# One full-width product per chunk operator in a bidirectional scan, instead of two half-width ones

## The chip, the cores and the metric

The kernel runs on one core of one Trainium2 chip. The metric is the time on the device in microseconds, from the program's first instruction to its end; several runs of the same program are taken and their median is compared.

## The reference, cut to what matters

One layer of a diffusion backbone is computed for 128 context tokens and 2048 latent tokens of width 1024. The input is normalised, modulated and multiplied by one wide input projection. Half of the channels (8 heads of 64) go through a recurrence with a 64 x 64 state per head, run once forward and once backward; the other half go through a short gated convolution; both halves meet in one output projection. The recurrence is what the change touches:

```python
def step(S, inp):
    r_t, w_t, k_t, v_t, kk_t, a_t = inp
    s_kk = jnp.einsum('bdhij,bdhj->bdhi', S, kk_t)
    S = (S * w_t[..., None, :] - s_kk[..., :, None] * (kk_t * a_t)[..., None, :]
         + v_t[..., :, None] * k_t[..., None, :])
    return S, jnp.einsum('bdhij,bdhj->bdhi', S, r_t)
...
s_final, ys = lax.scan(step, s0.astype(f32), xs)
```

## The kernel before, in words

The kernel has three phases. The first projects the inputs and writes the scan's operands to scratch memory. The second, the scan, is the one of interest. The third applies the output projection; its beginning is woven into the scan's end.

The scan works on chunks of 64 tokens. Within a chunk the recurrence is turned into matrix products, so that the state is carried from chunk to chunk by one product with an operator matrix of 128 x 128 for each head. A stage holds two groups, one per direction (`gi` and `d` are 0 for forward, 1 for backward), each of 8 chunks of one pair of heads. There are 17 stages; stage 15 is the context stage, whose groups hold two chunks of each of the four pairs.

For each stage and direction, in the names that the profile shows:

- `load_rr` (L998) and `load_sv` fetch operands and values; `load_stk` (L951) fetches one stack's lower half, tokens of 8 chunks for two heads, into partitions 0 to 63 of `stf`, `stg` or `sth`. These loads are issued on SyncE's queue, one DMA of 256 KB per stack in ordinary stages (L956) and four smaller ones per stack in the context stage (L959).
- `product` (L1021, tiles psGm, psQm, psFm) multiplies operands in 64 x 64 pieces; VectorE masks the results; GpSimd inverts small triangular matrices (`inverse`, L1081, tile zt); `merge` and `solve` (psU, psW, psX) build the rest of the inverse from them.
- `gcopies` (L1151) and `solve` (L1172) are ScalarE's writes of the stacks' upper halves, partitions 64 to 127.
- `operator` (L1174) multiplies the two stacks of a direction. One call makes the operators of two chunks and two heads in one tile, psE: for each of the four, two matmuls (L1186), one for each half of the 128 weight columns, writing partitions 0 to 63 and 64 to 127 of the result. A second call, "Ev", masks psE into E on VectorE (L1191).
- `state` (L1199, L1217, psS) applies E to the carried state with 64-column halves as weights; `scaled` (L1243) scales the new state on VectorE; the next chunk's psS waits for it. `outputs` and `finish` (psT at L1315, L1319, L1321) normalise and gate the output, with loads of `sg` and `w` (L1283) on SyncE.

A stack has two blocks (`b`, identity or copied rows), two heads (`h`) and eight chunks (`u`) of 64 tokens (`t`). Each direction has one `stf` tile, and one `stg` and one `sth` tile that alternate from stage to stage. The forward direction takes its weights from `stf` and its moving operand from `stg` or `sth`; the backward direction the other way round.

The order of instructions on TensorE, VectorE and ScalarE in the scan is written out by hand in the tables `SEQ` and `LATE`; GpSimd's and SyncE's orders are made by the scheduler. The words in these tables name a step, the two digits of its half and quarter, the direction and the stage distance: E000+1 is an operator product of the next stage. The change leaves the tables as they are.

In the order of TensorE's program there are 136 operator products in 82 runs. Of these runs 65 begin right after psS or psT and 17 after another tile; 64 end right before psS or psT.

The functions that the diff touches:

Of the kernel before, what the change touches and what calls it, by code (L numbers as in the profile page):

```python
# [6 lines left out]
F32 = mybir.dt.float32  # L7
# [808 lines left out]
def phase2(K):  # L816
    nc, tc, A, S = K.nc, K.tc, K.A, K.S
    V, G, P, T = nc.vector, nc.gpsimd, nc.scalar, nc.tensor
    D = nc.sync.dma_start
    MF, MG, ME = (0, 1), (0, 1), (2, 3)  # L820
    B = Ctx()
    O = Ctx()
    O.scaled = None

    def setup_first():

        O.r0 = Pool(K, "p2r0", "right")
        O.rI = Pool(K, "p2rI", "right")
        O.r1 = Pool(K, "p2r1", "right")
        O.pm = Pool(K, "p2m", "right", 2, PSUM)  # L830
        B.msk = O.r0.tile([128, 4, 128], F32, name="msk")
        B.mkg = O.r0.tile([128, 2, 128], F32, name="mkg")
        for i, j in enumerate((0, 2, 4, 5)):
            D(B.msk[:, i], A["msk"][:, j, 0:128])
        for i, j in enumerate((1, 3)):
            D(B.mkg[:, i], A["msk"][:, j, 64:192])
        B.I2 = O.r0.tile([128, 64], F32, name="I2")
        D(B.I2[:], A["i2"])
        B.idt = O.r0.tile([128, 128], F32, name="idt2")
        D(B.idt[:], A["idt"])  # L840
        B.hm = O.r0.tile([128, 2], F32, name="hm")
        D(B.hm[:], A["cst"][:, 514:516])
        B.ph = O.r0.tile([128, 3], F32, name="ph")
        D(B.ph[:], A["cst"][:, 516:519])
        B.slots = []
        for i in range(2):
            new_slot(O.r0)
        B.rr = ring(O.r1, 2, [128, 5, 8, 64], "rr", presetR)

    def new_slot(pool):  # L850
        i = len(B.slots)
        B.slots.append([tuple(pool.tile([128, 8, w], F32, tag=f"{n}{i}{d}", name=f"{n}{i}{d}", bufs=1) for n, w in (("F", 128), ("GA", 128), ("Q", 64))) for d in range(2)])
# [8 lines left out]
    def setup_rest():  # L861
        O.l0 = Pool(K, "p2l0", "left")
        O.l1 = Pool(K, "p2l1", "left")
        O.pS = Pool(K, "p2S", "left", 4, PSUM)
        O.p2 = Pool(K, "p2s", "left", 2, PSUM)
        O.r2 = Pool(K, "p2r2", "right")
        new_slot(O.r2)
        cp = O.l0
        vec = cp.tile([128, 4], F32, name="vec2")
        D(vec[:], A["vec"][:, V_GW:V_GW + 4])  # L870
        B.gwh = cp.tile([128, 4], F32, name="gwh")
        V.tensor_scalar(B.gwh[:], vec[:], 0.5, None, ALU.mult)
        B.geps = cp.tile([128, 1], F32, name="geps")
        V.memset(B.geps[:], 64e-5)
        B.pc = cp.tile([64, 2, 8, 34], F32, name="pc")
        for d in range(2):
            D(B.pc[:, d], S[f"pc{d}"].rearrange("(e c) n -> c e n", c=64))

        B.fs = ring(O.l1, 2, [128, 2, 2, 8, 64], "stf", presetS)
        B.gs = ring(O.l1, 2, [128, 2, 2, 8, 64], "stg", presetS)  # L880
        B.gs2 = ring(O.r2, 2, [128, 2, 2, 8, 64], "sth", presetS)
        B.zb = O.l1.tile([128, 16, 64], F32, name="zb")
        zero(B.zb)

    def ring(pool, n, shape, name, init=None):
        l = [pool.tile(shape, F32, name=f"{name}{i}") for i in range(n)]
        if init:
            for t_ in l:
                init(t_)

        def get():
            l.append(l.pop(0))
            return l[-1]
        get.tiles = l
        return get

    def copy(k, dst, src, negate=False):
        if negate:
            if k in ON_DVE:
                V.tensor_scalar(dst, src, -1.0, None, ALU.mult)  # L900
            else:
                P.activation(dst, src, AF.Copy, scale=-1.0)
        else:
            (V.tensor_copy if k in ON_DVE else P.copy)(dst, src)

    def zero(t_):
        G.memset(t_[:], 0.0)
# [6 lines left out]
    def presetS(t_):  # L914
        for hd in range(2):
            V.tensor_copy(t_[0:64, 0, hd], B.I2[0:64].unsqueeze(1).broadcast_to((64, 8, 64)))

    def tl(shape, tag, b, pool=None, dt=F32):
        return (pool or O.l0).tile(shape, dt, tag=tag, name=f"{tag}_{K.u()}", bufs=b)
# [29 lines left out]
    H0, H1, FULL = slice(0, 64), slice(64, 128), slice(0, 128)  # L949

    def load_stk(t_, g, k):  # L951

        p, c0 = g.units[0]
        src = S[f"ops{g.d}"][k]
        if p == g.units[-1][0]:
            D(t_[0:64, 1].rearrange("c h u t -> c h (u t)"), src[p * 128:p * 128 + 128, c0 * 64:(c0 + 8) * 64].rearrange("(h c) t -> c h t", h=2))  # L956
            return
        for i in range(4):
            D(t_[0:64, 1, :, 2 * i:2 * i + 2].rearrange("c h u t -> c h (u t)"), src[i * 128:i * 128 + 128, c0 * 64:(c0 + 2) * 64].rearrange("(h c) t -> c h t", h=2))  # L959

    def half(g, n):

        h = n if g.d == 0 else 1 - n
        return slice(h * 4, h * 4 + 4)
# [28 lines left out]
    def psum(name, s, shape):  # L993

        pool, tag = pool_of(name, s)
        return pool.tile(shape, F32, tag=tag, name=f"ps{name}_{s}_{K.u()}")
# [132 lines left out]
    def load_fs(s, st, gi):  # L1129

        g = st.g[gi]
        g.fs = B.fs.tiles[gi]
        load_stk(g.fs, g, 2)

    def load_gs(s, st, gi):

        g = st.g[gi]
        g.gs = (B.gs2 if s % 2 and s < NST - 3 else B.gs).tiles[gi]
        load_stk(g.gs, g, 1)
# [34 lines left out]
    def operator(name, s, st, gi):  # L1174

        g = st.g[gi]
        n, h2 = (int(c) for c in name[-3:-1])
        us = half(g, n)
        k = (h2 if g.d == 0 else 1 - h2) * 2
        if name[:2] != "Ev":  # L1180
            lt, rt = (g.fs, g.gs) if g.d == 0 else (g.gs, g.fs)
            pe = g.ps[name] = psum(name, s, [128, 2, 2, 128])
            for i in range(2):
                for hd in range(2):
                    for b, r in enumerate((H0, H1)):
                        T.matmul(pe[r, i, hd, :].rearrange("p (b t) -> p b t", b=2), lt[:, b, hd, us.start + k + i], rt[:, :, hd, us.start + k + i], start=True, stop=True)  # L1186
            return
        if n not in g.E:
            g.E[n] = tl([128, 4, 2, 128], f"E{n}{gi}", 1)
        pe = g.ps.pop("E" + name[-3:])  # L1190
        V.tensor_tensor(g.E[n][:, k:k + 2].rearrange("p a b c -> p (a b) c"), pe[:].rearrange("p a b c -> p (a b) c"),  # L1191
                        B.msk[:, ME[g.d]].unsqueeze(1).broadcast_to((128, 4, 128)), ALU.mult)
# [138 lines left out]
    def ending(name, s, st, gi):  # L1331
# [3 lines left out]
        if st.fin is not None:  # L1335
            next(st.fin, None)

    DO = dict(Gm=product, Qm=product, Fm=product, Ge=m_evict, Qe=m_evict, Fa=m_evict, Fe=m_evict, dg=diag, ab=turn, zi=begin, pre=pre, I=inverse,
              zr=zrows, zd=zrows, c0=zcopies, c1=zcopies, U=merge, bu=merge, W=merge, n=merge, gh=gcopies, X=solve, Xc=solve,
              E=operator, Ev=operator, S=state, sv=scaled, y=outputs,  # L1340
              fw=ending, fr=ending, fq=ending, fm=ending, T=ending, fy=ending, fa=ending)
    LOAD = dict(L=load_rr, gsL=load_gs, fsL=load_fs, svL=load_sv)
# [40 lines left out]

    def main():
        setup_rest()
        for b, n, t in order_of(range(-3, 0)):
            K.body = b
# [222 lines left out]
def build(nc, tc, A, outs):  # L1610
    K = Ctx()
    K.nc, K.tc, K.A = nc, tc, A
    n = [0]

    def u():
        n[0] += 1
        return n[0]

    K.u = u
    K.S = dict(outs)  # L1620
    for name, shape in {**SCR, **SCR2, "gate": (2, 1024)}.items():
        if name not in K.S:
            K.S[name] = tc.dram_tile(list(shape), F32, name=f"scr_{name}")[:]
    K.S["wsp"] = tc.dram_tile([34, 128, 2, 8, 128], F32, name="scr_wsp")[:]
    phase3(K)
    phase2(K)
    phase1(K)
    K.main()
# [18 lines left out]
```

## Time and profile before

| what | value |
|---|---|
| median of 3 runs | 1623.51 us (1619.18 to 1625.04) |
| the profiled execution | 1630.73 us |
| its span, first to last instruction | 1629.0 us |
| mean granted TensorE clock | 0.972 |
| scan, first stretch | 970 to 1345 us of the span |
| scan, its end with the context stage | 1345 to 1430 us |
| VectorE busy in the span | 70% |
| ScalarE, GpSimd busy in the span | 47%, 34% |

How to read the rows that follow: in the table of busy times a row is a stretch in microseconds, its length, and for each engine the busy time and, in brackets, the number of records; after them stand the granted clock, the share of the DMA engines and GB/s. In the chain and the timeline a row is a start, a length, the engine, the line and the tile, and how many records were merged into it. A form such as 128\*64 says how many rows and columns of weights a matmul uses. A float32 matmul leaves two records. The ends of matmuls are modelled, so starts and the ends of groups tell more than one record's length. "issue" is time in which an engine waited for nothing that the profile shows.

### The profile page before, as it was taken

How to read it: one execution, taken by the hardware profiler on the slowest of the kernel's cores; microseconds unless marked ns; L12 is line 12 of the kernel's file. 1: busy time of each engine (PE TensorE's matmuls, PEld its weight loads, DVE VectorE, ACT ScalarE, POOL GpSimd, SP SyncE). 2: the span in 40 equal slices, each digit the busy share in tenths (PEclk: the TensorE clock that was granted, in tenths of full speed). 3: DMA queues.
4: the chain of work that ended last, by engine and by line, in shares of the span. 5: the costliest groups of instructions: out<-in, count | busy, mean ns of one | idle time of the engine just before them, and what ended most of it. 6: DMA issues, size and time to landing. Idle time of an engine off the chain costs nothing.

```text
span 1629.0 us, 41750 instructions
## 1 busy us (share of the span) xinstructions
PE 1515.5 (93%) x17364; PEld 1402.4 (86%) x17364; DVE 1139.8 (70%) x1960; ACT 773.2 (47%) x1494; POOL 557.5 (34%) x961
## 2 busy tenths in 40 slices
PE   5899989999999999999999988999899897699998
PEld 2799989999999998999999987888788786578786
DVE  5899994764999636369975257897888886446533
ACT  4466652433555213145631047877687677322222
POOL 0033330001333000023315417787678866113221
PEclk8899999999999999999999979999999998799999
DMA  9559998663878765358886545565667645355442
GB/s 373 202 149 270 262 270 308 222 223 109 215 219 233 236 230 178 114 163 233 258 241 225 207 110 143 159 194 147 158 179 203 152 139 162 103 166 175 138 147 96
DMA packets 204589, 313.94 MB, mean 193 GB/s; under 512 B 58088, under 2 KB 147560, under 8 KB 190320
## 3 DMA queue, kind: packets, MB, share of 16 engines
q1 hardware_dynamic: 168816, 311.13, 61.9%
q10 hardware_dynamic: 35584, 0.14, 1.4%
q8 instruction: 136, 2.23, 0.6%
q14 instruction: 53, 0.43, 0.1%
HBM read 208.05 MB, written 103.17 MB: 191 GB/s over the span
## 4 chain that ended last, share of the span: by engine, by line
PE 64%; DVE 16%; DMA 9%; issue 6%; ACT 2%; SPq 1%; POOL 1%; ACTq 0%; DVEq 0%; POOLq 0%
PE psE L1186 6%; PE psu L1501 4%; PE psS L1217 3%; PE psu L1502 3%; PE psu L1503 3%; DMA scr_ops<-xs 2%; PE psFm L1019 2%; PE psX L1168 2%; PE mmb L182 2%; PE mmb L184 2%; PE mmb L183 2%; PE mmu L182 2%; PE mmu L184 2%; PE mmu L183 2%; PE mmgb L183 2%
## 5 line engine op out<-in xcount | busy, mean ns | idle before, releaser
L1091 POOL TENSOR_TENSOR zt<-zt,ztmp 128x30 f32<-128x30 f32 (+7 forms) x510 | 209.5, 411 | 39.7
L1088 POOL TENSOR_TENSOR ztmp<-ab,zt 128x60 f32<-128x60 f32 (+7 forms) x255 | 134.8, 529 | 104.5 <-DVE ab L1079 80.6
L1217 PE MATMUL psS<-sv,E 128*64 128x64 f32 x2176 | 103.1, 229 | 25.0 <-DVE so L1243 13.5
L1217 PEld LDWEIGHTS psS<-sv,E 128*64 128x64 f32 x2176 | 84.9, 140 | 43.9 <-issue 15.4
L410 POOL TENSOR_TENSOR sh<-rawl 128x384 f32<-128x384 f32 (+1 forms) x48 | 46.7, 991 | 210.6 <-ACT rawl L401 210.6
L1191 DVE TENSOR_TENSOR E<-psE,msk 128x512 f32<-128x512 f32 x136 | 91.0, 684 | 18.6 <-PE psE L1186 18.2
L1243 DVE TENSOR_TENSOR sv<-psS,pc 64x128 f32<-64x128 f32 x254 | 64.2, 275 | 45.1 <-PE psS L1217 43.6
L1566 POOL TENSOR_TENSOR z<-z,x 128x512 f32<-128x512 f32 x32 | 42.7, 1338 | 151.0 <-DVE z L1560 87.5
L1172 ACT ACTIVATE stf<-psX 64x512 f32<-64x512 f32 x136 | 80.4, 591 | 14.7 <-PE psX L1168 12.4
L434 POOL TENSOR_TENSOR hsl<-sq,hsh 128x384 fp32r<-128x384 f32 (+1 forms) x24 | 33.2, 1383 | 142.7 <-ACT hsh L429 137.0
L182 PE MATMUL mmg<-h,w 128*128 128x384 f32 (+1 forms) x216 | 70.8, 328 | 0.0
L183 PE MATMUL mmg<-h,w 128*128 128x384 f32 (+1 forms) x216 | 70.7, 327 | 0.0
L184 PE MATMUL mmg<-h,w 128*128 128x384 f32 (+1 forms) x216 | 70.6, 327 | 0.0
L182 PE MATMUL mmb<-h,w 128*128 128x384 f32 (+1 forms) x192 | 63.2, 329 | 6.0 <-ACT w L150 3.4
L182 PE MATMUL mmv<-h,w 128*128 128x384 f32 (+1 forms) x192 | 63.7, 332 | 3.8 <-ACT lf L665 3.1
L219 POOL TENSOR_TENSOR hslq<-ssq,hshq 128x384 fp32r<-128x384 f32 (+1 forms) x4 | 4.8, 1206 | 175.9 <-ACT hshq L218 112.0
L182 PE MATMUL mmc<-h,w 128*128 128x384 f32 (+1 forms) x192 | 63.7, 332 | 0.1
L184 PE MATMUL mmc<-h,w 128*128 128x384 f32 (+1 forms) x192 | 63.1, 329 | 0.3 <-DVE w L154 0.3
L184 PE MATMUL mmv<-h,w 128*128 128x384 f32 (+1 forms) x192 | 63.2, 329 | 0.0
L183 PE MATMUL mmv<-h,w 128*128 128x384 f32 (+1 forms) x192 | 63.1, 329 | 0.0
L183 PE MATMUL mmc<-h,w 128*128 128x384 f32 (+1 forms) x192 | 63.0, 328 | 0.0
L182 PE MATMUL mmu<-h,w 128*128 128x384 f32 (+1 forms) x192 | 62.7, 327 | 0.3 <-DMA w<-scr_wsp 0.3
(311 smaller groups left out, 5061.1 us busy)
## 6 DMA issues: line engine op xcount, KB each, us to landing
w<-scr_wsp SPq DMA_DIRECT2D x68, 1024.0 KB, 5.6
scr_wsp<-w SPq DMA_DIRECT2D x34, 1024.0 KB, 6.1
rr<-scr_ops SPq DMA_DIRECT2D x32, 1024.0 KB, 5.7
scr_ops<-xs SPq DMA_DIRECT2D x160, 192.0 KB, 6.2
wr<-in_win SPq DMA_DIRECT2D x34, 512.0 KB, 6.6
x<-in_x SPq DMA_DIRECT2D x17, 512.0 KB, 3.9
wadas<-in_wada SPq DMA_DIRECT2D x8, 1024.0 KB, 13.7
sv<-scr_vt SPq DMA_DIRECT2D x32, 256.0 KB, 3.7
```

Of the source, the lines that this page charges most:

```text
L182: T.matmul(ps[:, :n], w[:, 0, k], hh[:, 0, k, :n], start=k == 0, stop=False)
L183: T.matmul(ps[:, :n], w[:, 0, k], hh[:, 1, k, :n], start=False, stop=False)
L184: T.matmul(ps[:, :n], w[:, 1, k], hh[:, 0, k, :n], start=False, stop=k == 7)
L1088: G.tensor_tensor(tv, ab[:, j:j + 2, j + 2:32].unsqueeze(1).broadcast_to((128, kn, 2, n)), zt[:, :kn, j:j + 2].unsqueeze(3).broadcast_to(( ...
L1091: G.tensor_tensor(zt[:, :kn, j + 2:32], zt[:, :kn, j + 2:32], tv[:, :, r], ALU.subtract)
L1172: P.activation(g.fs[64:128, :, hd, e::2], g.ps["X"][e][hr_].rearrange("p a (b t) -> p b a t", b=2), AF.Copy, scale=-1.0)
L1186: T.matmul(pe[r, i, hd, :].rearrange("p (b t) -> p b t", b=2), lt[:, b, hd, us.start + k + i], rt[:, :, hd, us.start + k + i], start=True, ...
L1191: V.tensor_tensor(g.E[n][:, k:k + 2].rearrange("p a b c -> p (a b) c"), pe[:].rearrange("p a b c -> p (a b) c"), B.msk[:, ME[g.d]].unsquee ...
L1217: T.matmul(g.sp[i // 4][r, q, hd, :], g.E[n][:, k, hd, r], g.sv[:, u, hd, :], start=True, stop=True)
L1243: V.tensor_tensor(dst, g.sp[i // 4][0:64, q], B.pc[0:64, d, 2 * p:2 * p + 2, c:c + 1].broadcast_to((64, 2, 64)), ALU.mult)
L1501: T.matmul(ps[:], mh[:, n], hi[:, cs], start=start and n == 0, stop=False)
L1502: T.matmul(ps[:], mh[:, n], lo[:, cs], start=False, stop=False)
```

## The change

For each operator, one matmul with all 128 weight columns takes the place of the two with 64. Its weights must lie in one run of 128 elements per partition, so the tile that holds weights (`stf` of the forward direction, `stg` and `sth` of the backward one) is laid out anew: the two blocks of 64 tokens of a chunk stand side by side. A new helper, `stacks`, makes the tiles and hands out views with the old order of axes, so that the writers need no change. The lower half of such a tile is loaded in pieces of 256 bytes instead of 2 KB, by two DMAs, one per head. In the context stage all stacks, of either layout, are loaded by twice as many DMAs.

```diff
@@ -876,9 +876,9 @@
-        B.fs = ring(O.l1, 2, [128, 2, 2, 8, 64], "stf", presetS)
-        B.gs = ring(O.l1, 2, [128, 2, 2, 8, 64], "stg", presetS)
-        B.gs2 = ring(O.r2, 2, [128, 2, 2, 8, 64], "sth", presetS)
+        B.fs = stacks(O.l1, "stf", 0)
+        B.gs = stacks(O.l1, "stg", 1)
+        B.gs2 = stacks(O.r2, "sth", 1)
@@ -893,6 +893,19 @@
+    def stacks(pool, name, lhs):
+
+        c = Ctx()
+        c.tiles = []
+        for i in range(2):
+            if i == lhs:
+                t_ = pool.tile([128, 2, 8, 2, 64], F32, name=f"{name}{i}")[:].rearrange("p h u b t -> p b h u t")
+            else:
+                t_ = pool.tile([128, 2, 2, 8, 64], F32, name=f"{name}{i}")[:]
+            presetS(t_)
+            c.tiles.append(t_)
+        return c
@@ -952,11 +965,16 @@
         src = S[f"ops{g.d}"][k]
+        if g.d == (k == 1) and p == g.units[-1][0]:
+            for h in range(2):
+                D(t_[0:64, 1, h], src[p * 128 + h * 64:p * 128 + h * 64 + 64, c0 * 64:(c0 + 8) * 64].rearrange("c (u t) -> c u t", t=64))
+            return
         if p == g.units[-1][0]:
             D(t_[0:64, 1].rearrange("c h u t -> c h (u t)"), src[p * 128:p * 128 + 128, c0 * 64:(c0 + 8) * 64].rearrange("(h c) t -> c h t", h=2))
             return
         for i in range(4):
-            D(t_[0:64, 1, :, 2 * i:2 * i + 2].rearrange("c h u t -> c h (u t)"), src[i * 128:i * 128 + 128, c0 * 64:(c0 + 2) * 64].rearrange("(h c) t -> c h t", h=2))
+            for h in range(2):
+                D(t_[0:64, 1, h, 2 * i:2 * i + 2], src[i * 128 + h * 64:i * 128 + h * 64 + 64, c0 * 64:(c0 + 2) * 64].rearrange("c (u t) -> c u t", t=64))
@@ -1182,8 +1200,7 @@
                 for hd in range(2):
-                    for b, r in enumerate((H0, H1)):
-                        T.matmul(pe[r, i, hd, :].rearrange("p (b t) -> p b t", b=2), lt[:, b, hd, us.start + k + i], rt[:, :, hd, us.start + k + i], start=True, stop=True)
+                    T.matmul(pe[:, i, hd, :].rearrange("p (b t) -> p b t", b=2), lt[:, :, hd, us.start + k + i].rearrange("p b t -> p (b t)"), rt[:, :, hd, us.start + k + i], start=True, stop=True)
```

On TensorE, this is the middle of the scan, stage 8's operator products (psE, with the moving operand and the weights behind the arrow) between state products of two directions and the next psGm; "64x128" is the result's partitions by columns. Before:

```order
L1186 MATMUL psE_8_1439_14058<-stf_9633,stg_9639 64x128 x8
L1217 MATMUL psS_0_0_14069<-sv_13461,E_1434_13996 64x64 x4
L1217 MATMUL psS_1_4_13967<-sv_13069,E_1403_13611 64x64 x4
L1186 MATMUL psE_8_1441_14088<-stg_9638,stf_9632 64x128 x8
L1217 MATMUL psS_1_4_13967<-sv_13069,E_1403_13611 64x64 x4
L1217 MATMUL psS_0_0_14069<-sv_13461,E_1434_13996 64x64 x4
L1186 MATMUL psE_8_1445_14116<-stf_9633,stg_9639 64x128 x8
L1186 MATMUL psE_8_1447_14127<-stg_9638,stf_9632 64x128 x8
```

And after, at the same place, where lines of the code have moved by 17:

```order
L1203 MATMUL psE_8_1439_13817<-stf_9635,stg_9641 128x128 x4
L1234 MATMUL psS_0_0_13824<-sv_13254,E_1434_13755 64x64 x4
L1234 MATMUL psS_1_4_13730<-sv_12880,E_1403_13388 64x64 x4
L1203 MATMUL psE_8_1441_13843<-stg_9638,stf_9632 128x128 x4
L1234 MATMUL psS_1_4_13730<-sv_12880,E_1403_13388 64x64 x4
L1234 MATMUL psS_0_0_13824<-sv_13254,E_1434_13755 64x64 x4
L1203 MATMUL psE_8_1445_13867<-stf_9635,stg_9641 128x128 x4
L1203 MATMUL psE_8_1447_13874<-stg_9638,stf_9632 128x128 x4
```

Every step stands where it stood; a product is four matmuls over all 128 partitions instead of eight over halves.

On SyncE, the queue of an ordinary stage, from the stack loads to the next stage's operands. Before:

```order
L956 DMA stg_9639<-scr_ops_59 64x2x512
L956 DMA stf_9633<-scr_ops_59 64x2x512
L956 DMA stf_9632<-scr_ops_57 64x2x512
L956 DMA stg_9638<-scr_ops_57 64x2x512
L1283 DMA w_14384<-scr_q 128x512
L1009 DMA rr_8377<-scr_ops_57 128x4x512
L1009 DMA rr_8378<-scr_ops_59 128x4x512
```

And after:

```order
L970 DMA stg_9641<-scr_ops_59 64x8x64 x2
L973 DMA stf_9635<-scr_ops_59 64x2x512
L970 DMA stf_9632<-scr_ops_57 64x8x64 x2
L973 DMA stg_9638<-scr_ops_57 64x2x512
L1300 DMA w_14117<-scr_q 128x512
L1027 DMA rr_8377<-scr_ops_57 128x4x512
L1027 DMA rr_8378<-scr_ops_59 128x4x512
```

The two stacks that hold weights take two issues each, ahead of the w and rr loads.

On SyncE again, the context stage after the change, where before 16 loads at L959, of the form 64x2x128, stood in the stretch from the first stf row to the second group of sv rows:

```order
L977 DMA stf_9632<-scr_ops_57 64x2x64 x4
L960 DMA sv_16598<-scr_vt 64x4x128 x2
L977 DMA stf_9632<-scr_ops_57 64x2x64 x4
L977 DMA stg_9638<-scr_ops_57 64x128 x8
L1342 DMA scr_mixT<-sg_16416 128x512
L977 DMA stf_9635<-scr_ops_59 64x128 x3
L1300 DMA sg_16674<-scr_sg 128x512
L977 DMA stf_9635<-scr_ops_59 64x128 x5
L977 DMA stg_9641<-scr_ops_59 64x2x64 x8
L960 DMA sv_16844<-scr_vt 64x4x128 x2
L957 DMA sv_16865<-scr_vt 64x8x128
L1300 DMA w_16962<-scr_q 128x512
```

The 32 loads stand ahead of the sv and w loads; behind them come the loads of the output projection's weights (L1466 before, L1483 after).

## The prediction

> **What bounds the kernel now.** I read the page first, then the chain of waits, then the scan's stretch of both, then single pieces of TensorE's work there. The profiled execution took 1630.73 us, of which the span is 1629.0; the median of the runs shown is 1623.51. Differences are worked out inside the profiled span and put on the median.
>
> ```profile
> PE 64%; DVE 16%; DMA 9%; issue 6%; ACT 2%; SPq 1%; POOL 1%; ACTq 0%; DVEq 0%; POOLq 0%
> ```
>
> TensorE carries 64% of the chain that ended last. The change sits in the scan, so the scan's own rows count: the busy table of its two stretches, for all work and then for the operator products (tile psE) alone, and the chain's shares in the first stretch.
>
> ```profile
> 970.00:1345.00 375.00, 339.75 (x9320) 307.66 (x9320) 313.91 (x627) 279.58 (x555) 286.30 (x642) 0.97 0.60 164
> ```
>
> ```profile
> 970.00:1345.00 375.00, 123.67 (x1920) 107.10 (x1920) 79.00 (x118) 0.97 0.60 164
> 1345.00:1430.00 85.00, 21.14 (x258) 18.50 (x256) 12.03 (x18) 0.84 0.49 143
> ```
>
> ```profile
> by line: PE psE L1186 20.9%; PE psS L1217 13.6%; issue 8.1%; PE psX L1168 7.6%; PE psFm L1019 7.6%; PE psGm L1019 5.9%; DVE E L1191 4.6%; PE psU L1116 3.4%; DVE GA L1035 3.4%; PE psQm L1019 3.2%; DVE ab L1060 2.9%; DVE y L1262 2.8%; DVE sv
> ```
>
> TensorE is busy 339.75 of 375 us; VectorE, 313.91, is next. The products have 1920 + 258 records (two stand in both stretches), twice the program's 1088 matmuls: a float32 matmul leaves two records. They hold 20.9% of 375 = 78.4 us of the chain. What one chunk stage looks like on the chain:
>
> ```profile
> 1209.45 0.62 PE psS L1217 x16
> 1210.07 0.88 PE psE L1186 x16
> 1210.94 0.26 PE psS L1217 x8
> ...
> 1214.21 1.02 PE psE L1186 x16
> 1215.24 0.47 PE psS L1217 x16
> 1215.70 0.88 PE psE L1186 x16
> 1216.58 0.46 PE psS L1217 x16
> 1217.04 3.50 PE psE L1186 x64
> 1220.54 0.46 PE psS L1217 x16
> 1221.00 0.88 PE psE L1186 x16
> 1221.88 1.03 PE psGm L1019 x32
> ```
>
> Start, length, work. TensorE runs without a gap, so here a longer operator product lengthens the kernel one for one. A product of 16 records takes 0.88 us, four in a row 3.50, so 0.875 each: 78.4 of the 120 x 0.875 = 105 us of the first stretch, three quarters, lie on the chain.
>
> **The halved matmuls.** The diff replaces eight matmuls of 64 weight columns per product by four of 128, each streaming the same 128 columns. That saves time only if the two 64-column matmuls now run one after the other. They don't, by a row of its line's group and three of the timeline:
>
> ```profile
> L636 PE MATMUL psgate<-gaterow,sel x4: 591/592/592, 611.1 to 664.0; 128*2 128x512 f32 x4
> ```
>
> ```profile
> 611.09 1.02 PE L636 MATMUL psgate<-gaterow,sel 128*2 128x512 f32 x2
> ```
>
> ```profile
> 547.58 1.06 PE L212 MATMUL psgr<-wgate,scp 128*32 128x512 f32 x6
> ```
>
> ```profile
> 1209.89 1.05 PE L1186 MATMUL psE<-sth,stf 128*64 128x128 f32 x16
> ```
>
> psgate is one float32 matmul alone: its two records, 0.59 us each, end 1.02 us after the first began, so a record of 512 columns occupies its part of the array for 0.43 us. psgr has three times as many records, in three column parts, in 1.06 us: the parts work side by side. By the same rate a record of 128 columns should take 0.43 / 4 = 0.107 us, and 0.875 / 16 = 0.055 is half of that: the two column halves of a product already run together, at 0.109 per pair.
>
> A full-width record then takes 0.107 to 0.11 for its columns. Its weights are twice as wide, so the load beside it could become the limit. The nearest row is the transposes of v, 128 x 128 weights under 128 columns:
>
> ```profile
> 94.60 0.49 PE L504 MATMUL psv<-idt,ov 128*128 128x128 f32 x3
> ```
>
> ```profile
> L504 PE MATMUL psv<-idt,ov x68: 270/272/273, 94.6 to 837.8; 128*128 128x128 f32 x68
> ```
>
> Three take 0.49, the last one 0.27 of it, so they follow each other every 0.11 us with their loads hidden. A product after the change is 8 records x 0.109 = 0.875 us, as now. I take 0 for this edit; its ends are one record at half that (rival 1) and a load that isn't hidden (rival 3).
>
> The Trainium skill's "TensorE: Matmul & The Clock Gate", section Measured speedup vs the span model, states 2.38 times for three column tiles, not 3. By that, as an estimate, a pair would take 3 / 2.38 = 1.26 full records, and the change would save a fifth of 136 x 0.875 = 119 us, 25 us before any loss. The rows above disagree: three parts of psgr took 1.06 us where one alone took 1.02.
>
> **The borders.** Today psE, psS and psT all work in halves (128*64). After the change psE uses the whole array, and each border with psS or psT becomes a change of shape. What that costs stands in the chain. Sixteen psS records take 0.47 after psE and 0.62 after psX (64*64): 0.15 to leave. A product takes 0.88 after psS and 1.02 after psGm: 0.14 to enter in halves. Entering the full array is dearer:
>
> ```profile
> 1418.56 0.43 PE psa L1501
> 1418.99 0.23 PE psa L1502
> ```
>
> These are the first two full-width records after a psE: 0.43 against 0.23, so 0.20 to enter. The Trainium skill's "TensorEngine Tiling (Array Packing)", section Key Properties, says a change of tiling mode drains the engine and gives no figure; by a drain that costs the same both ways, taken at the 0.15 of leaving, the sum below would be 129 x 0.15 = 19.4. The rows make entering dearer, which I read as the wider first load standing exposed, and the measurement decides.
>
> In TensorE's order there are 82 runs of products; 65 begin after psS or psT, 64 end before one, and 17 begin after another shape, where 0.14 is paid already and 0.20 will be. So 65 x 0.20 = 13.0, 64 x 0.15 = 9.6, 17 x 0.06 = 1.0: 23.6 us of TensorE time. Three quarters of products lie on the chain, but the rest has little slack beside an engine busy 339.75 of 375; between 0.75 and 1 I take 0.85: **20 us**.
>
> **Instructions.** 1088 records and their 1088 weight loads go. TensorE's gaps marked "issue" in the scan's first stretch:
>
> ```profile
> PE psFm L1019 <- issue: 6.8, 7, 1.6
> PE psQm L1019 <- issue: 6.6, 3, 3.2
> PE psE L1186 <- issue: 4.4, 4, 1.4
> PE psS L1217 <- issue: 4.2, 4, 1.9
> ```
>
> 22.0 us in 18 gaps of about a microsecond. Those between 1195 and 1290 us, counted over the trace's TensorE records, start whole multiples of 256 records apart, so I take them for instruction loads that came late. 13.4 us stand before the quick psFm and psQm records, which stay; of the 8.6 before psE and psS I take a quarter: **-2 us**, ends -12 and 0.
>
> **The loads.** Each stage's two weight stacks come as two DMAs in 256-byte pieces instead of one in 2 KB pieces, and the context stage's 16 loads become 32. Rows of the trace's table of transfers (size, us to landing), of SyncE's queue, of TensorE and of VectorE:
>
> ```profile
> stf<-scr_ops SPq DMA_DIRECT2D x32, 256.0 KB, 5.6
> ```
>
> ```profile
> 1221.21 1.58 SPq L956 DMA_DIRECT2D stf<-scr_ops  x2
> ...
> 1334.43 0.58 SPq L959 DMA_DIRECT2D stf<-scr_ops  x1
> ...
> 1352.33 0.54 SPq L1283 DMA_DIRECT2D w<-scr_q  x1
> ```
>
> ```profile
> 1234.77 1.05 PE L1186 MATMUL psE<-stg,stf 128*64 128x128 f32 x16
> ```
>
> ```profile
> 1357.14 0.67 DVE L1321 TENSOR_TENSOR sg<-sg,w 128x512 f32<-128x512 f32 x1
> ...
> 1367.29 1.05 DVE L1099 STREAM_TRANSPOSE zr<-zt 128x512 f32<-128x512 f32 x1 [2.56 <-POOL zt L1091]
> ```
>
> In an ordinary stage two more issues of 0.6 put 1.2 us ahead of the w and rr loads. The stf loads go out at 1221 to 1223, the product that needs the first direction's starts at 1234.77; with landings of 5.6 us some 6 us of cover are left, and pieces twice as slow would use it up. I take 0, upper end 1 us a stage for 16 stages. In the context stage 16 more issues, 9.6 us less some 3 of waiting in that queue, fall between 1334 and 1352. Behind them stand w, which L1321 needs, and two output-weight loads, whose splitting runs on VectorE just ahead of the zr transpose at 1367.29. L1321 would slip from 1357 to about 1365 and zr by 3 to 5 us; behind zr the chain goes on. I take **+3**, ends 0 and 9.
>
> The preset copies, ScalarE's writes into the new layout (still runs of 64 elements) and the moving operands keep their sizes: 0.
>
> **Sum:** 20 - 2 + 3 = 21 us, so 1651.7 against the profiled 1630.73 and **1644.5 us** on the median.
>
> **Rivals.**
> 1. The halves don't really overlap, or a full-width float32 record is quicker than 0.107: each record then costs 0.055, 1088 x 0.054 = 59 us go, 50 on the chain, and with the borders the time is 1623.5 - 50 + 21 = 1595. It decides at 0.09 a record (21 us = 0.85 x 1088 x 0.023). For it: no row has a full-width float32 product of many columns. Against it: psgate and psgr. Chance 0.06.
> 2. The borders are absorbed: only half lies on the chain (12 us), and thinner instruction traffic takes half of the 22 us of issue gaps (-11): 1624, with 1615 to 1632 around it. For: issue holds 8.1% of the chain. Against: the gapless stage above. Chance 0.13.
> 3. Full-width weight loads can't run beside the record before: 0.107 more for each of 1088, 116 us, 99 on the chain: 1743. Against it: psv's spacing. Chance 0.05. The same page of the Trainium skill, section What overlaps and what doesn't, says loads overlap only where the row groups differ, which here they never do; the psv row contradicts it.
>
> **How the numbers follow.** The forecast has 0.76. Its own range: low 0.6 of the borders, -6 for instructions and 0 for loads, 1623.5 + 8 = 1632; high 23.6, 0, 9 and 12 for loads of ordinary stages, 1668. To hold the time 8 times in 10 the range takes in most of rival 2: 1626 to 1668, with rivals 1 and 3 outside. This kernel's measurement tells about 0.5%, 8 us, from no change. Faster by more: rival 1 and a little of rival 2, 0.08. Same: the rest of rival 2, 0.11. Slower: the forecast and rival 3, 0.81.
>
> **What the profile after would show.** 1088 psE records as 128*128, TensorE's count down to about 16276; a product alone between psS about 1.08 us on the chain, four in a row 3.70, the psS behind them 0.62: the border step right. Products of 0.5 us: rival 1. Products of 1.7: rival 3. Issue gaps under 12 us: rival 2. The context stage's loads ending 6 to 10 us later relative to their start, with L1321 or zr waiting: the load step. Wrong altogether if psE's length between psS stays 0.88 and the time still moves.

## The result, and the profile after

The changed kernel took 1637.76 us in the median of 8 runs (1632.55 to 1644.67), the kernel before 1625.77 us on the same chip (8 runs, 1619.18 to 1629.4): a ratio of 1.0075 with a 95% interval of 1.0053 to 1.0098, or 12 us more (9 to 16). By the half per cent that this measurement can tell, the change is slower. The profiled executions spanned 1629.0 us before and 1638.0 after, 9 us apart; the first took 5 us more than its kernel's median, the second 2 us more.

The chain of the changed kernel, shares by engine: TensorE rose from 64% to 70%.

```profile
PE 70%; DVE 13%; DMA 8%; issue 5%; ACT 2%; SPq 2%; ACTq 0%; DVEq 0%
```

One stage of it on the chain (start, length, work), the counterpart of the stage in the prediction:

```profile
1265.81 0.62 PE psS L1234 x16
1266.42 1.09 PE psE L1203 x8
...
1276.33 0.62 PE psS L1234 x16
1276.95 3.77 PE psE L1203 x32
1280.72 0.61 PE psS L1234 x16
1281.33 1.09 PE psE L1203 x8
1282.42 1.09 PE psGm L1037 x32
```

A product alone between psS now takes 1.09 us (0.88 before), four in a row 3.77 (3.50), the psS behind a product 0.61 to 0.62 (0.47). So the borders are there.

The kernels are compared below over the **ordinary stages**, here from the first to the 112th eviction of an operator on VectorE. There are eight evictions a stage, so these are the first 14 stages; the loads of the context stage (stage 15) are issued behind them. The busy table over that stretch, before and then after (length, then busy time and count of TensorE, weight loads, VectorE, ScalarE and GpSimd, then TensorE's granted clock):

```profile
977.67:1327.48 349.81, 315.61 (x8764) 285.80 (x8762) 296.88 (x592) 261.74 (x519) 271.73 (x602) 0.98 0.61 166
```

```profile
977.78:1335.43 357.65, 330.83 (x7866) 294.13 (x7862) 300.46 (x593) 261.85 (x519) 259.33 (x602) 0.99 0.61 163
```

TensorE is busy 15.2 us longer, but the stretch is only 7.8 longer: its idle time fell from 34.2 to 26.8 us.

What came behind that. First SyncE's queue in the changed kernel while it issues the context stage's loads, then what VectorE waited for there (us in total, times, longest), then VectorE's work that waited and the transpose zr on which the chain goes on:

```profile
1341.95 2.69 SPq L977 DMA_DIRECT2D stf<-scr_ops  x4
...
1361.13 7.39 SPq L977 DMA_DIRECT2D stg<-scr_ops  x8
1368.63 1.19 SPq L960 DMA_DIRECT2D sv<-scr_vt  x2
1369.94 0.58 SPq L957 DMA_DIRECT2D sv<-scr_vt  x1
1370.62 0.57 SPq L1300 DMA_DIRECT2D w<-scr_q  x1
1371.28 0.86 SPq L1483 DMA_DIRECT2D woraw<-in_wout  x2
```

```profile
DVE sg L1338 <- DMA w<-scr_q: 8.3, 1, 8.3
```

```profile
1374.59 0.69 DVE L1338 TENSOR_TENSOR sg<-sg,w 128x512 f32<-128x512 f32 x1 [8.28 <-DMA w<-scr_q]
...
1382.16 1.04 DVE L1117 STREAM_TRANSPOSE zr<-zt 128x512 f32<-128x512 f32 x1
```

The load of w goes out 35.2 us behind the 112th eviction (1335.43); before it was 24.9 (1352.33 behind 1327.48). VectorE stands 8.3 us at L1338, where it didn't wait before (L1321), and zr starts 46.7 us behind that eviction instead of 39.8. So another 6.9 us were lost up to zr.

This zr is the 17th and last, one for each stage, so it belongs to stage 16, the ordinary stage behind the context stage; the expectations below call it the context stage's, and the 112th eviction the last of the 16 ordinary stages. In VectorE's order it stands ahead of the context stage's evictions, so these slip with it. The context stage's own zr starts 16.9 us behind the 112th eviction before and 17.9 after.

Then the start of the output projection, where the tile psa is computed, before and then after:

```profile
1418.40:1441.20 22.80, 20.31 (x95) 15.38 (x92) 10.02 (x18) 5.43 (x11) 1.38 (x2) 0.93 0.65 197
```

```profile
1432.10:1449.50 17.40, 17.40 (x90) 13.87 (x89) 10.07 (x18) 5.14 (x10) 0.11 (x1) 1.00 0.79 242
```

For the same 72 records of psa, and a few of its neighbours, the kernel before needed 22.8 us at a clock of 0.93, the changed one 17.4 at 1.00. That is where some 5 us came back: from the 129th eviction to the end it took 222.1 us before and 216.5 after. Three views of the kernel before show what it lost there: what TensorE waited for within psa, ScalarE's work that it waited for, and the stretch right behind:

```profile
PE psa L1501 <- ACT mhc L1488: 2.5, 1, 2.5
```

```profile
1435.35 0.62 ACT L1488 CAST mhc<-mxc 128x512 fp32r<-128x512 f32 x1 [6.68 <-DMA mxc<-scr_mixT]
```

```profile
1437.40:1440.60 3.20, 3.20 (x9) 2.52 (x8) 1.58 (x3) 0.00 (x0) 1.28 (x1) 0.50 0.58 166
```

TensorE waits for a cast on ScalarE, which waits for the load of mxc, and then runs 3.2 us at half the clock. In the changed kernel it does neither. So the spans' 9.0 us are 7.8 in the ordinary stages, 6.9 from there to zr, about -6 behind that, and a rest under half a microsecond.

### The profile page after: what moved, and what is told of

Same layout as the page of the kernel before. It is cut to its first block, busy times and chain, and to the rows that moved or that the text cites. A ratio compares the mean times of both kernels' runs of the same rounds, so it can differ in the third digit from the quotient of the medians.

```text
span 1638.0 us, 39662 instructions
## 1 busy us (share of the span) xinstructions
PE 1535.5 (94%) x16276; PEld 1415.5 (86%) x16276; DVE 1141.5 (70%) x1960; ACT 772.9 (47%) x1494; POOL 547.8 (33%) x961
## 4 chain that ended last, share of the span: by engine, by line
PE 70%; DVE 13%; DMA 8%; issue 5%; ACT 2%; SPq 2%; ACTq 0%; DVEq 0%
PE psE L1203 8%; PE psS L1234 5%; PE psu L1518 4%; PE psu L1519 3%; PE psu L1520 3%; PE psX L1186 2%; PE psGm L1037 2%; PE mmb L182 2%; PE mmb L184 2%; PE psFm L1037 2%; PE mmb L183 2%; PE mmc L182 2%; PE mmc L183 2%; PE mmc L184 2%; PE mmu L184 1%
## 5 line engine op out<-in xcount | busy, mean ns | idle before, releaser
L1109 POOL TENSOR_TENSOR zt<-zt,ztmp 128x30 f32<-128x30 f32 (+7 forms) x510 | 197.1, 386 | 39.8
L1234 PE MATMUL psS<-sv,E 128*64 128x64 f32 x2176 | 103.1, 231 | 28.8 <-DVE so L1260 13.1
L1234 PEld LDWEIGHTS psS<-sv,E 128*64 128x64 f32 x2176 | 79.8, 139 | 53.4 <-DVE sv L1260 15.0
L1583 POOL TENSOR_TENSOR z<-z,x 128x512 f32<-128x512 f32 x32 | 42.7, 1338 | 146.2 <-DVE z L1577 99.4
L434 POOL TENSOR_TENSOR hsl<-sq,hsh 128x384 fp32r<-128x384 f32 (+1 forms) x24 | 35.6, 1485 | 141.6 <-ACT hsh L429 141.6
```

The lines of the kernel that those rows point to most:

```text
L1109: G.tensor_tensor(zt[:, :kn, j + 2:32], zt[:, :kn, j + 2:32], tv[:, :, r], ALU.subtract)
L1234: T.matmul(g.sp[i // 4][r, q, hd, :], g.E[n][:, k, hd, r], g.sv[:, u, hd, :], start=True, stop=True)
```

## The experiments

My theory after this: the borders cost TensorE about what I had priced, a thinner instruction stream gave part of it back, and the context stage's loads cost as much again. Rivals: the borders are simply absorbed by slack, or the loads cost everything.

A single profile scatters: for the three kernels with unchanged operator products in the old order the ordinary stages took 349.8, 340.0 and 351.8 us. So besides the length two parts are given. All TensorE records of the stretch are taken by their starts; where two follow each other by more than 0.3 us, all but 0.11 of it counts as **gap**, and the rest is **continuous work**. The table sets all kernels side by side (e7 has no row, because its one profiled execution took 7326 us; e9 is the same kernel). "zr" is how long after the 112th eviction that last transpose started, "tail" the time from the 129th eviction to the end, all in us.

| kernel | ratio to before (95%) | ordinary stages | work | gaps | records per us of work | zr | tail |
|---|---|---|---|---|---|---|---|
| before | 1 | 349.8 | 308.9 | 40.9 | 28.4 | 39.8 | 222.1 |
| after | 1.0075 (1.0053-1.0098) | 357.6 | 324.8 | 32.9 | 24.2 | 46.7 | 216.5 |
| e1 halves, new loads | 1.0062 (1.0041-1.0083) | 340.0 | 304.4 | 35.6 | 28.8 | 47.1 | 222.2 |
| e2 context 24 loads | 1.0029 (1.0007-1.0051) | 351.5 | 324.7 | 26.8 | 24.2 | 40.8 | 218.0 |
| e3 all full width | 1.0035 (1.0014-1.0055) | 349.9 | 343.4 | 6.5 | 20.2 | 47.1 | 214.6 |
| e4 before, 32 loads | 1.0057 (1.0033-1.0081) | 351.8 | 309.0 | 42.8 | 28.3 | 45.7 | 221.7 |
| e5 fewer borders | 1.0362 (1.0318-1.0406) | 395.1 | 331.2 | 63.9 | 23.5 | 43.8 | 217.2 |
| e6 before, e5's order | 1.0254 (1.0218-1.0290) | 383.6 | 320.1 | 63.5 | 27.1 | 40.5 | 220.7 |
| e8 more borders | 1.0167 (1.0126-1.0209) | 375.9 | 340.6 | 35.4 | 24.4 | 42.7 | 217.2 |
| e9 = e7 full width, 24 loads | 0.9990 (0.9977-1.0003) | 348.7 | 342.9 | 5.8 | 20.2 | 41.5 | 215.2 |
| e10 before, psS full width | 1.0197 (1.0172-1.0222) | 376.3 | 363.1 | 13.2 | 21.8 | 42.4 | 217.3 |
| e11 e2 + 1088 quick records | 1.0271 (1.0246-1.0296) | 386.3 | 346.1 | 40.2 | 25.2 | 42.2 | 217.4 |
| e12 runs wide, others halved | 1.0059 (1.0039-1.0079) | 362.8 | 319.5 | 43.4 | 26.0 | 42.2 | 217.3 |

**e1: the changed layout and loads, halved products again.**

```diff
-    T.matmul(pe[:, i, hd, :]..., lt[:, :, hd, us.start + k + i].rearrange("p b t -> p (b t)"), ...)
+    for b, r in enumerate((H0, H1)):
+        T.matmul(pe[r, i, hd, :]..., lt[:, b, hd, us.start + k + i], ...)
```

> The changed kernel with its layout and its loads, but each operator product again as two products of 64 weight columns. Theory (the borders between the full-width products and the half-width psS cost the ordinary stages 7 to 8 us net, the context stage's 16 more loads about 7 us there, of which some 5 are given back behind the scan): the borders go, so the ordinary stages end where those of the kernel before do (last operator eviction of the 16 ordinary stages, 112 evictions after the first, 349 us behind the first instead of 356.7), the zr transpose of the context stage still comes some 7 us later after that than before; time 1626 to 1632, ratio to the kernel before 1.000 to 1.005. Rival (the 256-byte pieces and the extra loads cost all of it): as slow as the change, 1636 to 1639, ratio 1.006 to 1.009.

It came out at 1.0062: inside the rival's range, just above mine. Without full-width products nearly all of the loss is still there. Its trace says where: the ordinary stages show no loss (work 304.4, 340.0 in all), so the 256-byte pieces and the second DMA cost nothing there; zr is 7 us late, and the 5 us behind it don't come back (tail 222.2). So the products' net share of the change is small (1.0075 against 1.0062, about 2 us and not clear of noise), while the borders are plainly in the changed kernel's rows. The other runs settle how both can be.

**e4: the kernel before, with 32 context loads.**

```diff
     for i in range(4):
-        D(t_[0:64, 1, :, 2 * i:2 * i + 2].rearrange("c h u t -> c h (u t)"), ...)
+        for h in range(2):
+            D(t_[0:64, 1, h, 2 * i:2 * i + 2], ...)
```

> The kernel before, with nothing changed but the context stage's 16 stack loads split by head into 32 (same pieces, same layout). Theory of the queue: 16 more issues of 0.6 us less what that queue waits anyway, so the zr transpose of the context stage starts about 7 us later behind the last ordinary operator eviction (48 instead of 41 us), time 1625 to 1632, ratio 1.001 to 1.005. Rival (the loads are hidden): no shift of zr, ratio 0.998 to 1.002.

What VectorE waited for around its context loads, as in the changed kernel's view above:

```profile
DVE sg L1322 <- DMA w<-scr_q: 8.7, 1, 8.7
```

The wait for w appears without any other part of the change. zr is 5.9 us later than before, the time 9.2 us (5.3 to 13.1), just beyond what I expected. So the loads are not hidden.

**e2: the change, with 24 context loads.**

```diff
+    if g.d != (k == 1):
+        for i in range(4):
+            D(t_[0:64, 1, :, 2 * i:2 * i + 2].rearrange("c h u t -> c h (u t)"), ...)
+        return
     for i in range(4):
         for h in range(2):
```

> The changed kernel, but the context stage's eight stack loads of the moving operands come for both heads in one, as before (24 loads instead of 32; the weights' stay split). Theory that the queue of SyncE sets the context stage: 8 issues x 0.6 = 5 us less ahead of the output-weight load, so the zr transpose of the context stage starts some 5 us earlier behind the last ordinary operator eviction (43 instead of 48 us) and the end comes 0 to 5 us earlier, 1633 to 1638. Rival (something else holds zr): zr stays at 48 us and the time at 1638.

The same wait, and zr:

```profile
DVE sg L1342 <- DMA w<-scr_q: 2.0, 1, 2.0
```

```profile
1362.29 1.05 DVE L1121 STREAM_TRANSPOSE zr<-zt 128x512 f32<-128x512 f32 x1 [0.16 <-POOL zt L1113]
```

Eight issues fewer brought zr back to 40.8 us, where it waits for GpSimd's inverse as before, and the ratio from 1.0075 to 1.0029, 7 us, more than the 0 to 5 expected. So in these profiles the first eight extra issues cost 1 us up to zr and the second eight 6. Over all kernels of the table zr comes at 39.8 to 42.4 us with 16 loads, 40.8 to 43.8 with 24 and 45.7 to 47.1 with 32: most of the cost comes with the second eight.

**e3: psS and psT full width too.**

```diff
     for hd in range(2):
-        for r in (H0, H1):
-            T.matmul(g.sp[i // 4][r, q, hd, :], g.E[n][:, k, hd, r], ...)
+        T.matmul(g.sp[i // 4][:, q, hd, :], g.E[n][:, k, hd, :], ...)
```

The transposes of L1332 likewise.

> The changed kernel with the state products psS and the output transposes psT full width too (128 weight columns under 64 or 128 moving ones, half the matmuls), so that no border to psE is left; loads as changed. If borders are what the change lost in the ordinary stages and a full-width load hides beside 64 moving columns: psE 0.89 us behind psS, a psS product of 8 records 0.45, ordinary stages back at 349 us or under, time 1622 to 1632. If the 128-column load then sets the pace (0.107 a record): psS takes 0.86 instead of 0.46 a product, some +0.4 x 136 x 0.85 = 46 us less the borders' 20, about 1660. Rival (borders cost nothing): 1638 in the first case, 1684 in the second.

Both branches happened at once. psS's pace is the one that the second branch gave: the raw starts of its records, with 64 moving columns, lie 0.112 us apart, as psE's do with 128. Work rose by 18.6 us over the changed kernel in spite of the missing borders. But the gaps fell from 32.9 to 6.5 us, which neither theory had, and the time is 1.0035, 6.5 us under the change.

**e7 and e9: e3 with e2's loads.**

> The kernel of e3 (psE, psS and psT all full width) with e2's 24 context loads. Theory: the two parts add up: e3's 1.0035 less the 6 us that the zr transpose comes earlier (41 us behind the last ordinary operator eviction instead of 47), ratio 0.999 to 1.001; gaps over 0.3 us in the ordinary stages stay under 12 us (6.5 in e3, 27 to 33 with half-width psS). Rival (e3's missing gaps were chance): gaps of 20 us or more, ratio 1.004 or over.

> The kernel of e7 again, unchanged, since the profiled execution of e7 was disturbed and its trace can't be read. Theory as for e7: ratio 0.997 to 1.001; gaps over 0.3 us in the ordinary stages under 12 us, continuous work 343 us there, zr 41 us behind the last ordinary operator eviction. Rival (e3's missing gaps were chance): gaps of 20 us or more.

Both came out at 0.999 (e7 with 0.9969 to 1.0012, e9 as in the table). The busy table of e9's ordinary stages, and the first two rows of what TensorE waited for there (us in total, times, longest):

```profile
970.21:1318.94 348.73, 344.51 (x6941) 322.43 (x6936) 301.65 (x592) 261.94 (x519) 262.25 (x605) 1.00 0.62 167
```

```profile
PE psFm L1041 <- issue: 1.2, 1, 1.2
PE psQm L1041 <- issue: 0.9, 2, 0.5
```

The gaps are gone again (5.8 us), so e3's were no chance, and the two repairs add up: 1.0035 less 6 us. This is the best version with full-width products, and it is level with the kernel before, not better.

**e8: more borders.**

```diff
     for hd in range(2):
-        T.matmul(pe[:, i, hd, :]..., lt[:, :, hd, ...].rearrange("p b t -> p (b t)"), ...)
+        if i == 0:
+            T.matmul(pe[:, i, hd, :]..., lt[:, :, hd, ...].rearrange("p b t -> p (b t)"), ...)
+            continue
+        for b, r in enumerate((H0, H1)):
+            T.matmul(pe[r, i, hd, :]..., lt[:, b, hd, ...], ...)
```

> The kernel of e2 with the first half of each operator product full width and the second in halves (6 matmuls instead of 4 or 8): a product alone keeps its one entry and one exit, each of a run of products gets its own, 43 more of each in the ordinary stages. Theory (0.35 us a pair of borders): 15 us more continuous TensorE work there (about 340 after 324.7), some of it hidden, time 8 to 15 us over e2, ratio 1.008 to 1.012. Rival (borders mostly absorbed): ratio 1.003 to 1.006.

The busy table of its ordinary stages:

```profile
971.52:1347.44 375.92, 347.53 (x8320) 294.93 (x8320) 301.25 (x592) 261.81 (x519) 262.05 (x609) 0.99 0.59 155
```

Work rose by 15.9 us, as priced (15). The time rose by 22 us over e2 (14 to 30), and the gaps grew too, by 8.6: with halves come more records (8320 instead of 7866 in the changed kernel). So nothing shows that slack absorbs a border's cost.

**e5 and e6: operator products moved together, in the changed kernel and in the one before.**

```diff
-... S61+-1 Ge0+3 dg0+3 gh10+1 sv61+-1 E110 sv00 S71+-1 ... sv10 E111 ... E101 y11+-1 E011 ... S01 E100 ...
+... S61+-1 Ge0+3 dg0+3 gh10+1 sv61+-1 sv00 S71+-1 ... sv10 E110 E111 ... E101 y11+-1 E011 E100 ... S01 ...
-... S70 ... E000+1 sv70 fy Xc11+1 Ev000+1 zd+2 S51 gh01+2 U+2 y01 Gm0+4 E001+1 c0+2
+... S70 ... sv70 fy Xc11+1 zd+2 S51 gh01+2 U+2 y01 Gm0+4 E000+1 E001+1 Ev000+1 c0+2
```

> The kernel of e2 (the change with 24 context loads) with the order of the first 13 loop bodies rewritten so that operator products stand together: four entries and four exits a stage become two and two (three entries from psS and one from psGm before, now one from psS and one from psGm). Theory (a border costs 0.20 to enter and 0.15 to leave on TensorE, and about half of that comes through to the end): 0.7 us a stage x 13 = 9 us less continuous TensorE work over the ordinary stages (324.7 us without gaps in e2, so about 316), time 4 to 9 us under e2's 1.0029, ratio 0.997 to 1.000. Rival (borders are absorbed by waits): 316 too, but the gaps grow by as much, ratio 1.003. Second rival (the longer runs of products hold up the chain of state products): the gaps before psS grow by 5 us or more, ratio 1.003 to 1.008.

> The kernel before with the same rewritten order of the first 13 bodies and nothing else: the price of the order itself, without full-width products. Theory: in halves psE and psS pass into each other for some 0.05 us, so nothing is gained: continuous work 307 +- 3 us, ratio 0.998 to 1.002. If the longer runs hold up the state products: 1.002 to 1.008. If it falls to 0.995 or so the order is better by itself and e5's gain is not the borders'.

Both misses: 3.6% and 2.5% slower. The second rival's mechanism was at work, at several times the size that it gave. The first row of what TensorE waited for in e6's ordinary stages:

```profile
PE psS L1212 <- DVE sv L1238: 29.1, 31, 2.1
```

The longer runs stand in the way of the state products, which then wait for one another through VectorE; in the old order this wait was a tenth of that (2.5 us in the kernel before, from 970 to 1345 us). The two runs don't price borders: the order does more than the borders do.

**e10: the kernel before with psS alone full width** (e3's diff of psS, on the kernel before).

> The kernel before with only the state products psS full width (1088 matmuls fewer, as many as the change removed, but from the other side of the border); operator products in halves. Theory (a border costs the same from either side, a thinner instruction stream closes gaps whoever leaves it): continuous work of the ordinary stages 307 + 22 (psS at 0.107 a record) + 17 (borders) = 346 us, gaps over 0.3 us 30 or fewer instead of 36 to 43, no delay of zr (40 us); together 370 to 376 us behind the first eviction, ratio 1.010 to 1.018. Rival (the gaps have nothing to do with the number of instructions): gaps 36 to 43, ratio 1.019 to 1.025.

```profile
969.74:1346.07 376.33, 365.42 (x7906) 326.16 (x7901) 303.57 (x592) 262.16 (x519) 262.08 (x608) 0.99 0.55 155
```

Gaps fell to 13.2 us, far under the 30 that I had as a limit, though as many records are left as in the changed kernel (7906 and 7866). Work rose to 363, 17 us more than expected: psS has many more neighbours than psE, and by the starts of records psQm, psFm and psX now begin 0.205 us after its last record instead of 0.152. The ratio, 1.0197, lies in the rival's range, but for the wrong reason: work too large, gaps smaller still.

**e11: e2 with psW computed twice.**

```diff
-    for r0, r1 in rows:
+    for r0, r1 in rows * 2:
         T.matmul(pw[r0, u, :], st.zd[r1, u, :], B.zb[r1, u, 32:64], start=True, stop=True)
```

> The kernel of e2 (the change with 24 context loads) with each product of psW computed twice: 544 matmuls, 1088 records more, just as many as the change took away, at 0.019 us each. Theory (instruction gaps follow the number of TensorE instructions): continuous work of the ordinary stages 324.7 + 16.2 = 341 us and gaps over 0.3 us back from 27 to 36 or more, so the time 22 to 28 us over e2, ratio 1.016 to 1.020. Rival (the gaps don't follow it): gaps stay at 25 to 33, time 16 us over e2, ratio 1.011 to 1.014.

Its busy table, and two of TensorE's waits there:

```profile
971.21:1357.51 386.30, 352.98 (x8705) 316.24 (x8700) 300.60 (x592) 261.66 (x519) 257.80 (x599) 0.96 0.57 151
```

```profile
PE psQm L1041 <- issue: 8.7, 7, 1.9
PE psGm L1041 <- issue: 6.6, 5, 2.4
```

The gaps are back at 40.2 us, where the theory put them, and work is 346 (341 expected) at a clock that fell from 0.99 to 0.96. The time rose by 39 us over e2, more than either theory said.

**e12: full width only in the runs of four.**

```diff
-    T.matmul(pe[:, i, hd, :]..., lt[:, :, hd, ...].rearrange("p b t -> p (b t)"), ...)
+    if name[1:4] in ("111", "010", "101", "011"):
+        T.matmul(pe[:, i, hd, :]..., lt[:, :, hd, ...].rearrange("p b t -> p (b t)"), ...)
+        continue
+    for b, r in enumerate((H0, H1)):
+        T.matmul(pe[r, i, hd, :]..., lt[:, b, hd, ...], ...)
```

> The kernel of e2, but full width only for the four operator products of a stage that stand in a row (E111, E010, E101, E011); the four that stand alone beside psS are halves again. One entry and one exit a stage are left of four and four, 544 of the 1088 removed records stay removed, context loads 24. Theory: continuous work of the ordinary stages 307 + 16 x 0.35 + 1 = 314 us, gaps over 0.3 us between e2's and those of the kernel before, some 33, so 346 to 350 us; ratio 0.997 to 1.001, the best of the versions with full-width products. Rival (borders don't matter): as e2, 1.003.

```profile
970.35:1333.20 362.85, 326.07 (x8310) 293.13 (x8304) 299.28 (x593) 261.63 (x519) 264.79 (x605) 0.96 0.60 161
```

A miss: 1.0059. Work is 319.5 at a granted clock of 0.96, which at the 0.98 of the kernel before would be 313 by my estimate (319.5 x 0.96 / 0.98), so the borders seem to have gone as expected (314). But half of the instructions came back, and with them all the gaps (43.4).

## Why the prediction was right, and where not

The sign held and so did the range: 12 us slower against a forecast of 21, and 1637.8 us in 1626 to 1668. The total came about otherwise than forecast, and that it fell in the range is in part luck. The forecast gave 18 of its 21 us to the products (20 - 2) and 3 to the loads. By the medians the loads cost 9 to 10 us (e4, and e1 with the layout), and the products some 2 us on top, which is not clear of noise: the borders were there at their price, but shorter gaps and the end of the scan gave most of it back. Step by step:

- **The halved matmuls, 0 us: right.** A product alone is 1.09 us and not 0.5 or 1.7, so rivals 1 and 3 are out. The records follow each other every 0.112 us by their starts, instead of every 0.109 per pair: some 2 us that I didn't count. The loads of the full width run beside the record before, although their row groups are the same. That is against the rule of the Trainium skill that rival 3 cites; it stands in "TensorE: Matmul & The Clock Gate", under What overlaps and what doesn't.
- **The borders: size right, and their share of the path rather too low than too high.** Priced at 23.6 us for 136 products, so at 19 for the 111 of the ordinary stages; the work there rose by 17.3 (mean of 308.9, 304.4 and 309.0 against that of 324.8 and 324.7), some 2 of it by the spacing above. By starts, from the last psS record ahead of a lone product to the first behind it, it took 0.93 us before and takes 1.24 now: 0.31 for a pair of borders, the wider spacing included, where I had 0.35. In e9, where psS and psE are both full width, psE's first record starts 0.112 us after psS's last, no later than inside a product, and only its second is 0.05 us late. The Trainium skill's drain at a change of mode ("TensorEngine Tiling (Array Packing)", section Key Properties) agrees with these numbers. And e8 shows no slack that takes the borders up.
- **Instructions, -2 us: the step that failed.** It was a tenth of the gaps' 22 us, on the ground that most stand before quick records which stay. Between the same two groups of kernels the gaps fell from 39.8 to 29.9 us, by 10, close to my end of -12. e11 shows that records put back bring gaps back (40.2). That the pace at which instructions are used up decides, and not their number alone, fits e3, e9 (6.5 and 5.8) and e10 (13.2, with as many records as the changed kernel); but these three are also the ones with a full-width psS, and no run tells the two apart. This was half of my rival 2; its other half, borders absorbed, was not so. Net, the ordinary stages lost 7.4 us, 347.2 to 354.6, between means of single profiles of which the first three lie 12 us apart.
- **The loads, +3 us: the mechanism right, the size not.** L1321, now L1338, waits for w, and zr slips by 6.9 us, within my bounds of 0 to 9. I took 3 because I let zr slip less than L1321. L1338 starts 39.2 us behind the 112th eviction, where L1321 started after 29.7, so 9.5 later; zr follows in VectorE's order, and only the 2.6 us that it had waited for GpSimd before fall away: 6.9. The ordinary stages' loads cost nothing, as predicted (e1).
- **Not foreseen: 5 us given back behind the scan.** Before, e1, e4 and e6 lose 2.8 to 3.1 us within psa, from one record's start to the next, and then show six to eight of its records 0.43 us apart instead of 0.23, the rows at half the clock above. None of the kernels with any full-width psE or psS does both. What differs is the load of mxc: it is issued 7 us behind psa's first record in all kernels, but ScalarE's cast starts 9.7 to 9.9 us after that in these four, 8.1 in e10 and 5.6 to 7.4 in the others. Why the load is slower there stays open.

So 7.4 + 6.9 - 5 gives 9 us where the forecast had 21; the runs' medians say 12, with the 9 to 16 of their interval, and the profiles of the two kernels lie 5 and 2 us over their medians.

## What to carry to other kernels

Halving the number of matmuls saved nothing here, where their halves already ran side by side; it saves instructions, and whether those matter is read from TensorE's "issue" gaps, not from its busy time. A change of tile shape in a densely interleaved stream has a price at each border, and it can be read off the chain before the change is made: a run's length behind its own kind against its length behind another. And a layout that needs twice as many DMAs is paid where their queue is on the path: for one stage in seventeen here, and by the runs' medians that cost more than the products did net.

## What the runs showed of the hardware

- **TensorE's instruction gaps go with the pace, steeply.** In the old order, with 20 to 22 records per us of work the ordinary stages had 6 to 13 us of gaps, with 24 to 29 they had 27 to 43, without a trend inside the second group; all kernels of the first have a full-width psS. In e11 the seven gaps over 0.7 us between 1118 and 1238 us begin 512, 768, 1280, 1280, 512, 768 and 768 instructions (matmuls, weight loads and the few semaphore instructions among them) after the gap before, each within one of a multiple of 256. The Trainium skill's "Runtime: NRT & Kernel Launch", section Instruction fetch mechanics, says that instructions come in blocks of 256 and that fetching them is hidden, or mostly so. The multiples agree with the first half; the gaps, 40.2 us in 386.3 there, speak against the second if fetching is their cause. That a block that comes late is the cause is what these numbers suggest; no run took the blocks themselves apart.
- **Where gaps are many the granted clock is lower too:** 0.96 in e11 and e12 against 1.00 in e9's ordinary stages.
- **A full-width float32 record is not faster with 64 moving columns than with 128:** 0.112 us between starts either way (psE in the changed kernel, psS in e3). That fits a weight load which sets the pace; no run varied the load alone.
- **Leaving a full-width psS costs more than leaving a half-width one:** the next psQm, psFm or psX record starts 0.205 us after the first (e10) and 0.152 after the second, though both have 64 moving columns; from psE, with 128, to psGm it is 0.20 in either width.
